# Ranking fourteen experts by load, and giving the six smallest 64-slot steps of plain float32 products

## The chip, the cores and the metric

The kernel runs on one core of one Trainium2 chip. The metric is the device time of one execution in microseconds. The median of three runs of the kernel before is 1223.13 us (1218.1 to 1224.14).

The engines are named as the profile names them: PE multiplies matrices (PEld loads its stationary operands), DVE, ACT and POOL work on elements, SP issues most DMAs. A partition is one of the 128 rows of on-chip memory.

## The reference

A trunk of two layers over 512 tokens of 1024 float32 values. Each layer adds a mixer (layer 0: retention and a state-space model, layer 1: dilated attention; the change touches neither) and then a mixture of 16 experts:

```python
    gval, gsel = lax.top_k(jax.nn.softmax(glog, axis=-1), 1)
...
    elog_sel = jnp.take_along_axis(elog, gsel[:, :, None], axis=1)[:, 0]
    top_v, top_i = lax.top_k(elog_sel, TOP_K)
    top_w = jax.nn.softmax(top_v, axis=-1) * gval
...
    for g in range(N_GROUPS):
        h = jax.nn.silu(jnp.einsum('td,edf->tef', t, w_gate[g])) * jnp.einsum('td,edf->tef', t, w_up[g])
        out = out + jnp.einsum('tef,efd->td', h * combine[:, g, :, None], w_down[g])
```

`glog` and `elog` are the logits of the four groups and of their four experts each. Every token goes to two of the 16 experts, both of one group, so an expert has 64 tokens on average. With the inputs that the reference draws, the 16 experts of layer 0 get 61, 51, 65, 79, 47, 45, 49, 49, 81, 64, 83, 70, 81, 52, 79 and 68 tokens, those of layer 1 get 66, 56, 48, 56, 51, 52, 43, 68, 88, 103, 91, 82, 47, 52, 67 and 54. An expert has three matrices of 1024 x 512 (gate, up) and 512 x 1024 (down), each 2 MB in float32 and read as two loads of 1 MB: 96 loads a layer.

## The kernel before

**Routing.** While the mixer's output projection still runs, the router's logits are worked out chunk by chunk (128 tokens each). `route` then gives each token its place among the rows of its expert (`pos`). `listed(e)` (L966 to L977) turns `pos` into the list of expert e's rows: DVE compares (`oh`, L966), eight short PE products (L972, L973), and a DVE copy to `idx` (L975). A branch (L1270, L1271) sends all work to `moe_any` (every expert over all 512 tokens) if an expert has more than 128 rows.

**Steps.** `moe` (L1086) then runs experts 0 to 15 in the order of their numbers, one step each, always with 128 slots. A step gathers the expert's rows (`fetch`, L1112, an indirect DMA on POOL, issued two steps ahead), turns them with eight transposes into `X` as two tiles (`split_to`, L174), and multiplies in `proj` (L1140 to L1170) by up, then by the next expert's gate, then in `down` by down. Every product is made of three float32r products of 128x512 (`mm3`, L177 to L179): high by high, high by low, low by high. For that every weight block is split: ACT rounds it to the high part, DVE subtracts to get the low part (`wsplit`, with L174). A step so has 24 products, 72 PE instructions of 512 columns, and 12 splits of 128x1024 each on ACT and DVE. `gate` ends in a Silu on ACT (L1174), and L1295 multiplies by up on DVE. The result leaves PSUM on ACT (L1215), and POOL scatters it by an indirect DMA into the rows of `Yd` in HBM (L1216).

**Weights.** SP issues the loads in program order (`load_w`, L235) into a ring of 12 slots of 1 MB, two experts' worth; a load waits until the splits of the slot's last weights are done. The address is constant, the expert's number being known. 14 of a layer's loads are issued before the branch. The second half of up(2) is loaded by POOL (L1154).

**Tail.** Experts 14 and 15 are not scattered: their results stay on chip as high and low parts in `X[0]`, `X[1]`, and `add_rows` (L1237) adds them to `h` by products with one-hot tables, four for each half chunk. The other experts' rows come back from `Yd` by eight loads (L1259) after the last scatter has landed; POOL adds six of them to `h` in layer 0 and four in layer 1 (L1261), DVE and, in layer 1, PE (L1240) the rest.

Of the kernel before, what the change touches and what calls it, by code (L numbers as in the profile page):

```python
# [21 lines left out]
T = 512  # L22
D = 1024
NCH = 4
# [12 lines left out]
C_ID, C_TRI, C_IOTA, C_ZETA, C_TL, C_TIE, C_SEL, C_END = 0, 128, 256, 384, 388, 389, 405, 425  # L37
# [3 lines left out]
def _constants():  # L41
    """Tables that depend on shapes alone."""
# [8 lines left out]
    for i in range(20):  # L51
        cst[i::32, C_SEL + i] = 1.0
    half = 64
# [19 lines left out]
    return {"cst": cst, "tab0": np.ascontiguousarray(tab0), "tab1": np.ascontiguousarray(tab1)}  # L73
# [3 lines left out]
def kernel(ctx: ExitStack, tc: tile.TileContext, I, out, *_):  # L77
# [110 lines left out]
    def sumsq(src, junk, first):  # L188
        """Sums of squares of 512 columns; the first half's is taken with the mean's scale and eps."""
# [12 lines left out]
    scaled, recips = [], []  # L202
# [39 lines left out]
    def wsplit(raw, eng=V):  # L242
        """raw [128, 2, 512]: hi and lo."""
# [43 lines left out]
    def outproj(parts, src, done):  # L287
        """h[t, :] += sum over the two parts (hi, lo, row0) of merged[t, :] src; done(c) after chunk c."""
# [31 lines left out]
    # ---------------------------------------------------------------- layer 0  # L320
# [21 lines left out]
    def s5_tables(st, ld, db, Br, Cn):  # L342
# [36 lines left out]
        M8 = sm.tile([128, 8, 3, 16], F32, bufs=1, name="M8")  # L379
# [92 lines left out]
    def s5_in(hf, W, U, X):  # L472
        """Chunk inputs to states of half hf."""
# [10 lines left out]
    def s5_scan(P, hf, X):  # L484
# [4 lines left out]
        def swap(v):  # L489
            """im before re."""  # L490
# [3 lines left out]
        def step(dst, src, m, n):  # L494
            """dst += lam^(8(m+1)) src; [128, 2, 8, n] views."""
# [243 lines left out]
    # ---------------------------------------------------------------- layer 1  # L739
# [61 lines left out]
    # ---------------------------------------------------------------- mixture of experts  # L801
# [14 lines left out]
    def router_params(l, eng=nc.scalar):  # L816
# [9 lines left out]
        def scaled():  # L826
            """The norm's weights times the router's."""
# [7 lines left out]
    def router(l, wr, br, wrb):  # L835
        grow = rowb(I["ffn_norm"][l])

        def t4(name, *shape, dt=F32):
            return sm.tile([128, NCH] + list(shape), dt, bufs=1, name=name)

        q = SimpleNamespace(r=t4("rank", 5, 4), gs=t4("gs", 4), M=t4("M", NE, dt=BF16), E=[t4(f"E{k}", NE) for k in range(2)],
                            pos=t4("pos", NE), pp=bank(shape=(128, NCH + 1, NE)), oh=t4("oh0", 128, dt=BF16),
                            idx=sm.tile([128, NE, 2], I32, bufs=1, name="idx"), ohf=[], xn=[])
        part = {}

# [6 lines left out]
        def ranks(c):  # L852
            """Rank 3 is the largest of its four, rank 2 the next; the lower index first."""
# [26 lines left out]
        def rows0():  # L880
            """Rows of expert 0 out of the first two chunks; zeros where it has none."""
# [16 lines left out]
        def chunk(c, n):  # L898
            """Half n of chunk c: transposed now, multiplied behind the next half's transposes."""
# [50 lines left out]
    def route(q):  # L950
        M, E, pp, pos, chosen = q.M, q.E, q.pp, q.pos, q.chosen
        for c in range(NCH):
# [8 lines left out]
        def listed(e, part=range(5), oh=None):  # L961
            """Rows of expert e: where they are read from and written to (too large: no row), and their weights."""
            if oh is None:
                oh = ohr[listed.n if listed.n < 2 else 2 * (listed.n % 2)]
                listed.n += 1
                V.tensor_tensor(oh, C[:, C_IOTA:C_IOTA + 128][:, None, :].to_broadcast([128, NCH, 128]),  # L966
                                pos[:, :, e:e + 1].to_broadcast([128, NCH, 128]), op=OP.is_equal)
# [6 lines left out]
            if 0 in part:  # L974
                V.tensor_scalar(idx[:, e, :], pl2[:, 0:2], float(FAR), None, op0=OP.add)  # L975
            if 4 in part:
# [3 lines left out]
        def weights():  # L980
# [28 lines left out]
            V.tensor_tensor(wt, wt, r, op=OP.add)  # L1009
            V.tensor_copy(rc[:, :, :, 2], wt)  # L1010
# [5 lines left out]
        return idx, cmax, M, E, listed, weights, ws  # L1016
# [69 lines left out]
    def moe(l, rt, norm, done):  # L1086
        idx, cmax, M, E, listed, weights, ws = route(rt)
        Yd = Yds[l]
        xg = [F[9][:, 0:1024], F[9][:, 1024:2048]]
# [4 lines left out]
        X, hb = [R[g0]], []  # L1094

        def rest():
            """What the first loads leave: the other expert's rows and the products' operand."""
            X.append(typed(once[0:1], F32R)[0])
# [4 lines left out]
            R[once[0]] = X[1]  # L1103

        def xgb(e):
            return [v3(X[e % 2][:, 1024 * i:1024 * i + 1024], 8) for i in range(2)]
# [3 lines left out]
        def fetch(e):  # L1110
            x_ = xg[e % 2]
            rows[e] = G.indirect_dma_start(out=x_, out_offset=None, in_=xnd[:, :],  # L1112
                                        in_offset=bass.IndirectOffsetOnAxis(ap=idx[:, e, 0:1], axis=0),
                                        bounds_check=T - 1, oob_is_err=False)
# [258 lines left out]
```

## Time and profile before

| | |
|---|---|
| median of three runs | 1223.13 us |
| profiled execution: span | 1223.2 us (no other time of that execution is given) |
| expert steps, layer 0 / layer 1 | 299 to 630 us / 889 us to the end |
| PE, DVE, ACT, POOL busy | 93%, 77%, 60%, 18% of the span |
| DMA, whole span | 284.39 MB, mean 233 GB/s |

The span is the time from the first instruction to the last; it equals the median within 0.1 us. The busy shares are averages over stages with different limits. The two stretches of expert steps are together over half of the span, and the change lies within them, so their rows are read by themselves below.

### The profile page before, as it was taken

What the parts mean: (1) busy time and instruction counts of PE and PEld (TensorE: products, weight loads), DVE (VectorE), ACT (ScalarE), POOL (GpSimd) and SP (SyncE); (2) the same over time, 40 slices, a digit from 0 to 9 for tenths busy, and PEclk for the clock granted to TensorE, in tenths of its full rate; (3) what the DMA queues carried; (4) which work ended last, traced back from release to release, by engine and by line L of the source; (5) the groups of instructions that cost most, each with busy time, mean ns of one, the idle gap of its engine ahead of it and who ended that gap; (6) DMA issues with size and microseconds to landing.
All of it is one profiled execution on the core that took longest, in us unless ns stands there. A gap on an engine that the chain in (4) does not pass through costs nothing. (4 is left out here: it accounts for less than half of the span.)

```text
span 1223.2 us, 16929 instructions
## 1 busy us (share of the span) xinstructions
PE 1135.8 (93%) x6271; PEld 902.6 (74%) x6271; DVE 939.3 (77%) x1497; ACT 729.0 (60%) x1029; POOL 214.4 (18%) x138
## 2 busy tenths in 40 slices
PE   6989797998899999999699999999889999999976
PEld 5767676886678888887468877777667888888754
DVE  5974865766999999988983273275589999999896
ACT  6342144534878888878453353453368888878764
POOL 3553010001211101110620000000032111022041
PEclk9989998998999999999989999999889999999998
DMA  7255532387889999988615314317468999999661
GB/s 240 86 154 203 208 88 94 104 295 232 308 296 342 367 373 351 379 304 278 239 39 173 103 36 172 104 35 258 162 230 307 337 365 371 373 363 382 234 248 69
DMA packets 135745, 284.39 MB, mean 233 GB/s; under 512 B 25067, under 2 KB 25251, under 8 KB 135524
## 3 DMA queue, kind: packets, MB, share of 16 engines
q1 hardware_dynamic: 120564, 248.71, 58.0%
q0 software_dynamic: 9328, 18.63, 4.4%
q10 hardware_dynamic: 5760, 15.86, 3.4%
q8 instruction: 53, 0.87, 0.3%
q14 instruction: 40, 0.33, 0.1%
HBM read 268.74 MB, written 30.41 MB: 245 GB/s over the span
## 5 line engine op out<-in xcount | busy, mean ns | idle before, releaser
L178 PE MATMUL acc<-R,R 128*128 128x512 f32 x1204 | 484.6, 403 | 20.0 <-DVE R L174 19.1
L174 DVE TENSOR_TENSOR R<-F,R 128x1024 fp32r<-128x1024 f32 (+1 forms) x281 | 354.7, 1283 | 127.2 <-ACT R L174 118.0
L177 PE MATMUL acc<-R,R 128*128 128x512 f32 x1084 | 440.7, 408 | 6.7 <-ACT R L174 4.8
L179 PE MATMUL acc<-R,R 128*128 128x512 f32 x1084 | 428.4, 400 | 0.2 <-DVE R L174 0.2
L174 ACT CAST R<-F 128x1024 fp32r<-128x1024 f32 (+1 forms) x284 | 294.6, 1047 | 198.8 <-PE acc L179 102.5
L178 PEld LDWEIGHTS acc<-R,R 128*128 128x128 f32 x1204 | 229.6, 191 | 75.3 <-DVE R L174 26.9
L177 PEld LDWEIGHTS acc<-R,R 128*128 128x128 f32 x1084 | 206.9, 191 | 59.7 <-ACT R L174 15.4
L179 PEld LDWEIGHTS acc<-R,R 128*128 128x128 f32 x1084 | 207.2, 191 | 45.7 <-DVE R L174 1.3
L1112 POOL DMA_INDIRECT F<-xnd,idx x30 | 49.8, 1661 | 346.1 <-DVE idx L975 182.5
L174 DVE TENSOR_TENSOR R<-pb,R 128x512 fp32r<-128x512 f32 x120 | 81.7, 686 | 32.0 <-ACT R L174 31.8
L174 DVE TENSOR_TENSOR R<-R,R 128x1024 fp32r<-128x1024 f32 x70 | 90.2, 1317 | 5.7 <-ACT R L174 5.2
L174 ACT CAST R<-R 128x1024 fp32r<-128x1024 f32 x70 | 72.4, 1053 | 35.9 <-PE acc L179 34.8
L174 ACT CAST R<-pb 128x512 fp32r<-128x512 f32 x120 | 69.8, 589 | 33.9 <-PE pb L170 30.8
L174 DVE TENSOR_TENSOR R<-F,spare 128x1024 fp32r<-128x1024 f32 x58 | 75.1, 1296 | 1.6 <-ACT spare L174 1.5
L174 ACT CAST spare<-F 128x1024 fp32r<-128x1024 f32 x62 | 65.2, 1051 | 9.6 <-PE acc L179 9.2
L179 PE MATMUL acc<-spare,R 128*128 128x512 f32 x180 | 70.9, 394 | 0.0
L177 PE MATMUL acc<-spare,R 128*128 128x512 f32 x180 | 70.5, 392 | 0.0
L1216 POOL DMA_INDIRECT Yd<-m,idx x28 | 35.0, 1252 | 100.8 <-ACT m L1215 94.0
L883 POOL MEMSET R<- 128x1024 f32 x2 | 1.9, 958 | 284.4 <-PE acc L179 284.4
L170 PE MATMUL pb<-C,F 128*128 128x128 f32 x296 | 45.0, 281 | 4.0 <-POOL F L460 3.4
L170 PEld LDWEIGHTS pb<-C,F 128*128 128x128 f32 x296 | 36.2, 145 | 10.7 <-POOL F L460 3.9
L170 PE MATMUL pb<-C,m 128*128 128x128 f32 x164 | 28.4, 295 | 15.3 <-DVE m L207 9.9
(331 smaller groups left out, 1304.7 us busy)
## 6 DMA issues: line engine op xcount, KB each, us to landing
F<-in_moe_w_gate_dram SPq DMA_DIRECT2D x58, 1024.0 KB, 9.1
F<-in_moe_w_down_dram SPq DMA_DIRECT2D x46, 1024.0 KB, 6.8
F<-in_moe_w_up_dram SPq DMA_DIRECT2D x36, 1024.0 KB, 5.0
R<-in_moe_w_up_dram SPq DMA_DIRECT2D x24, 1024.0 KB, 10.2
R<-in_moe_w_down_dram SPq DMA_DIRECT2D x18, 1024.0 KB, 5.7
F<-in_c_w_qkv_dram SPq DMA_DIRECT2D x12, 1024.0 KB, 5.1
F<-in_ab_w_in_dram SPq DMA_DIRECT2D x10, 1024.0 KB, 5.1
Yd<-h ACTq DMA_DIRECT2D x16, 512.0 KB, 4.0
```

What stands on the lines that cost most here:

```text
L170: PE.transpose(dst, src, ident[:n, :n])
L174: return S.copy(hi, src), eng.tensor_tensor(lo, src, hi.bitcast(F32), op=OP.subtract)
L177: PE.matmul(ps, ah, bh, start=first, stop=False)
L178: PE.matmul(ps, ah, bl, start=False, stop=False)
L179: PE.matmul(ps, al, bh, start=False, stop=last)
L883: G.memset(q.x0, 0.0)
L1112: rows[e] = G.indirect_dma_start(out=x_, out_offset=None, in_=xnd[:, :], in_offset=bass.IndirectOffsetOnAxis(ap=idx[:, e, 0:1], axis=0), b ...
L1216: st = G.indirect_dma_start(out=Yd[:, :], out_offset=bass.IndirectOffsetOnAxis(ap=idx[:, e, 1:2], axis=0), in_=y[:, :], in_offset=None, bo ...
```

## The change

`STEPS = "HHHLHHLHLHHLHHLL"` gives each of the 16 steps a kind. Experts 0 and 1 keep the first two steps. The 14 others are ranked on chip by their number of rows: the eight largest go to the heavy steps (H), which are computed as before, the six smallest to the light steps (L: 3, 6, 8, 11, 14, 15), which have 64 slots. The branch to `moe_any` is now also taken if more than eight of the 14 have more than 64 rows.

**Ranking.** `loads` works out the counts and the branch's condition, and PE turns `pos` and `E[1]` together into a transposed tile. After the branch `by_load` ranks the counts on DVE, and two PE products with the resulting permutation give `ids` (the expert's number of each step) and the permuted `pos`. SP reads `ids` into 14 registers; each weight load of a step from 2 on takes its address from one (an ISA instruction ahead of the DMA). The loads of gate(2), issued before the branch so far, now wait for that, and the whole of up(2) is issued by SP.

**Light steps.** Rows are gathered and transposed with 64 partitions. PE's products take float32 operands as they are, with no split of weights or rows. Each is 64 rows by 512 columns, and two at a time are issued to the two column halves of the array: up into PSUM partitions 0 to 63 and gate into 64 to 127 (L1282); the left and the right 512 columns of down (L1302). The scatter writes half rows of 2 KB (L1359).

**Tail.** Steps 14 and 15 are light. Their results stand side by side in one pair of tiles `Z`, 64 slots each, so that `add_rows` has two products where it had four. The four slots that take the rows coming back are now the last four of the ring.

```diff
+STEPS = "HHHLHHLHLHHLHHLL"
...
+            V.tensor_scalar(m14, pp[:, 4, 2:NE], LIGHT + 0.5, CAP / NHEAVY, op0=OP.is_gt, op1=OP.mult)
+            V.tensor_reduce(more, m14, AX.X, OP.add)
+            V.tensor_tensor(cf, cf, more, op=OP.max)
+            V.tensor_copy(cmax, cf)
...
+        def by_load(bT):
+            cnt, rank, own, gt, P = srt[:, 186:187], srt[:, 187:188], srt[:, 142:158], srt[:, 158:172], srt[:, 192:304]
+            V.tensor_tensor(own, srt[:, 112:128], pp[:, 4, :], op=OP.mult)
+            V.tensor_reduce(cnt, own, AX.X, OP.add)
+            V.scalar_tensor_tensor(gt, pp[:, 4, 2:NE], cnt, srt[:, 128:142], op0=OP.subtract, op1=OP.is_gt)
+            V.tensor_reduce(rank, gt, AX.X, OP.add)
+            V.tensor_scalar(P, srt[:, 0:112], rank, None, op0=OP.is_equal)
+            pi = bank(shape=(1, NS))
+            PE.matmul(pi, C[0:64, C_EC:C_EC + 1], P[0:64, 0:NS], start=True, stop=True)
+            ids = srt[0:1, 304:304 + NS].bitcast(I32)
+            V.tensor_copy(ids, pi)
+            pm = bank(shape=(128, 2, NCH, NS))
+            PE.matmul(pm.rearrange("p x c s -> p (x c s)"), bT, P, start=True, stop=True)
+            V.tensor_copy(pos[:, :, 2:NE], pm[:, 0])
...
+            return wv[w][bass.ds(ids[e], 1), r0:r1, :].rearrange("e (k p) n -> p (e k) n", p=128)
...
         def gate(e):
             hs = m2([128, 512], "hs")
-            return hs, S.activation(hs, proj(e, "moe_w_gate"), AF.Silu)
+            if STEPS[e] == "H":
+                return hs, S.activation(hs, proj(e, "w_gate"), AF.Silu)
+            x_, ps = light_x(e), bank(psA, name="acc")
+            for kk in range(2):
+                raw = [load(e, w, kk * 512, kk * 512 + 512) for w in ("w_up", "w_gate")]
+                for k in range(4):
+                    for i in range(2):
+                        PE.matmul(ps[LIGHT * i:LIGHT * i + LIGHT], x_[:, 4 * kk + k, :], raw[i][:, k, :],
+                                  start=kk + k == 0, stop=kk + k == 4, skip_group_check=True)
...
+        def light_down(e, hs):
...
+            for kk in range(2):
+                raw = load(e, "w_down", kk * 256, kk * 256 + 256)
+                for k in range(2):
+                    for i in range(2):
+                        n = 1 - i if flip else i
+                        PE.matmul(ps[LIGHT * i:LIGHT * i + LIGHT], ht[:, 2 * kk + k, :],
+                                  raw[:, k, 512 * n:512 * n + 512], start=kk + k == 0, stop=kk + k == 2,
+                                  skip_group_check=True)
...
+            y = m4([128, 512], "y")
+            S.activation(y, ps, AF.Copy, scale=ws[:, e:e + 1])
+            scattered(G.indirect_dma_start(out=Yh[:, :],
+                                           out_offset=bass.IndirectOffsetOnAxis(ap=idx[:, e, 1:2], axis=0),
+                                           in_=y[:, :], in_offset=None, bounds_check=4 * T - 1, oob_is_err=False))
...
-                    PE.matmul(ps, sel[b][:, c, :], X[b][:, 1024 * i + 512 * n:1024 * i + 512 * n + 512],
-                              start=b == 0 and i == 0, stop=y2 is None and b == 1 and i == 1)
+            for i in range(2):
+                PE.matmul(ps, sel[n][:, c, :], Z(n, i), start=i == 0, stop=y2 is None and i == 1)
...
-                spare.extend(order[5:6] + order[1:4])
-                fr.set(order[0:1] + order[4:5] + order[6:])
+                spare.extend(order[8:12])
+                fr.set(order[0:8])
```

SP's row of instructions before, from the end of the branch in layer 0 (tiles of F and R are slots of the ring, m4, growt and m2w take up(2)):

```order
L1271 UNCONDITIONAL_BRANCH
L1151 DMA m4_0_90<-in_moe_w_up_dram 128x2x512
L1151 DMA growt_107<-in_moe_w_up_dram 128x2x512
L235 DMA F0_70<-in_moe_w_gate_dram 128x4x512
L235 DMA F2_72<-in_moe_w_gate_dram 128x4x512
L235 DMA F3_73<-in_moe_w_down_dram 128x2x1024
```

And SP's row of the changed kernel from the same place:

```order
L1415 UNCONDITIONAL_BRANCH
L1424 TENSOR_LOAD srt_2029
L1177 ISA
L1177 DMA F8_78<-in_moe_w_gate_dram 128x4x512
L1177 ISA
L1177 DMA R3_2494<-in_moe_w_gate_dram 128x4x512
L1253 ISA
L1253 DMA m4_0_90<-in_moe_w_up_dram 128x2x512
L1253 ISA
L1253 DMA growt_107<-in_moe_w_up_dram 128x2x512
L1255 ISA
L1255 DMA m2w_87<-in_moe_w_up_dram 128x4x512
```

The read of `ids` and the two loads of gate(2) now stand ahead of the loads of up(2), and each load has an ISA instruction ahead of it.

PE's row before in layer 0 at the end: the last products of down(15), and the first of `add_rows` (R6, R4, R7 are high and low weights, R2, R0 the results of experts 14 and 15, R1 the operand and the one-hot tables):

```order
L177 MATMUL acc_5275<-R4_2877,R1_2954 128x512
L178 MATMUL acc_5275<-R4_2877,R1_2954 128x512
L179 MATMUL acc_5275<-R4_2877,R1_2954 128x512
L1237 MATMUL acc_5344<-R2_82,R1_2954 128x512 x2
L1237 MATMUL acc_5344<-R0_2953,R1_2954 128x512 x2
L1237 MATMUL acc_5350<-R2_82,R1_2954 128x512 x2
```

And PE's row of the changed kernel at the same place, from the last up and gate products of step 15 on (F are the ring's slots as loaded, R0 the turned rows, m2w the operand of down):

```order
L1282 MATMUL acc_4842<-F3_73,R0_4826 64x512
L1282 MATMUL acc_4842<-F4_74,R0_4826 64x512
L1302 MATMUL acc_4873<-F7_77,m2w_87 64x512 x4
L189 MATMUL pb_4890<-C_92,m2w_87 128x64 x4
L1302 MATMUL acc_4873<-F5_75,m2w_87 64x512 x4
L1302 MATMUL acc_4896<-F6_76,m2w_87 64x512 x4
L1302 MATMUL acc_4896<-F1_71,m2w_87 64x512 x4
L1384 MATMUL acc_4944<-R2_4884,R1_3002 128x512
L1384 MATMUL acc_4948<-R2_4884,R1_3002 128x512 x2
```

PE now reads the weights as they were loaded, with no split between the landing and the products. Behind step 15's up and gate products stand only the sixteen products of down(14) and down(15), then `add_rows`; up(15) and down(15) alone were 48 rows before.

## Rows read from the trace of the kernel before

**Rows 1.** The page: busy time by engine, and GB/s of 40 slices of the span.

```profile
PE 1135.8 (93%) x6271; PEld 902.6 (74%) x6271; DVE 939.3 (77%) x1497; ACT 729.0 (60%) x1029; POOL 214.4 (18%) x138
GB/s 240 86 154 203 208 88 94 104 295 232 308 296 342 367 373 351 379 304 278 239 39 173 103 36 172 104 35 258 162 230 307 337 365 371 373 363 382 234 248 69
```

**Rows 2.** Stretches: us, busy PE, PEld, DVE, ACT, POOL (count), clock, DMA share, GB/s.

```profile
375.00:523.00 148.00, 147.43 (x735) 119.73 (x734) 137.32 (x151) 122.41 (x144) 21.50 (x17) 1.00 1.01 366
523.00:585.20 62.20, 61.98 (x287) 49.14 (x287) 54.46 (x58) 49.87 (x60) 6.11 (x4) 1.00 0.81 283
964.00:1112.00 148.00, 147.42 (x740) 120.62 (x739) 137.93 (x153) 123.10 (x145) 22.66 (x18) 1.00 1.01 369
1112.00:1174.60 62.60, 62.39 (x291) 49.87 (x290) 55.23 (x58) 50.52 (x60) 6.12 (x4) 1.00 0.80 284
493.80:499.00 5.20, 5.20 (x29) 4.20 (x28) 5.05 (x5) 4.95 (x7) 0.00 (x0) 1.00 1.05 399
```

**Rows 3.** POOL's timeline, two scatters of neighbouring steps: start, us, what, idle before.

```profile
427.45 1.01 POOL L1216 DMA_INDIRECT Yd<-m,idx  x1 [0.30 <-issue]
...
446.02 1.00 POOL L1216 DMA_INDIRECT Yd<-m,idx  x1 [0.31 <-issue]
```

**Rows 4.** PE's timeline within a step, three products in a row.

```profile
444.38 0.39 PE L178 MATMUL acc<-R,R 128*128 128x512 f32 x1
444.61 0.39 PE L179 MATMUL acc<-R,R 128*128 128x512 f32 x1
```

**Rows 5.** PE's timeline: float32 products of 512 columns in layer 1's mixer.

```profile
708.03 1.02 PE L759 MATMUL pb<-F,F 128*128 128x512 f32 x2
708.89 0.61 PE L779 MATMUL pb<-m2w,F 128*128 128x128 f32 x4
```

**Rows 6.** PE's timeline: float32 products on column halves (128*64), layer 0's mixer.

```profile
100.60 3.97 PE L479 MATMUL pb<-F,F 128*64 128x64 f32 x128
```

**Rows 7.** PE's timeline: from a full-width product to products on 32 columns.

```profile
281.32 0.39 PE L179 MATMUL acc<-R,R 128*128 128x512 f32 x1
281.64 0.43 PE L917 MATMUL pb<-m,wrb 128*32 128x128 f32 x8
```

**Rows 8.** DMA issues on the page: count, KB each, median us to landing.

```profile
F<-in_moe_w_gate_dram SPq DMA_DIRECT2D x58, 1024.0 KB, 9.1
```

**Rows 9.** DVE's timeline behind layer 0's branch.

```profile
299.05 0.69 DVE L966 TENSOR_TENSOR m2w<-C,pos 128x512 bf16<-128x512 f32 x1 [2.84 <-PEq L1271]
299.66 0.15 DVE L975 TENSOR_SCALAR idx<-pb 128x2 int32<-128x2 f32 x1
```

**Rows 10.** PE's timeline, end of layer 0's steps, with waits.

```profile
599.54 0.50 PE L178 MATMUL acc<-R,R 128*128 128x512 f32 x1 [1.67 <-DVE R L174]
...
611.24 1.11 PE L170 MATMUL pb<-C,m 128*128 128x128 f32 x4 [3.62 <-DVE m L1295]
...
613.62 0.63 PE L178 MATMUL acc<-R,R 128*128 128x512 f32 x1
614.05 0.63 PE L177 MATMUL acc<-R,R 128*128 128x512 f32 x1
...
621.07 6.13 PE L1237 MATMUL acc<-R,R 128*128 128x512 f32 x26
...
629.31 0.40 PE L177 MATMUL acc<-R,R 128*128 128x512 f32 x1
```

**Rows 11.** POOL's timeline, end of layer 0's steps.

```profile
577.46 1.83 POOL L1216 DMA_INDIRECT Yd<-m,idx  x1 [19.36 <-ACT m L1215]
588.98 6.11 POOL L1261 TENSOR_TENSOR h<-h,F 128x1024 f32<-128x1024 f32 x2 [9.69 <-DMA F<-Yd]
...
601.69 6.68 POOL L1261 TENSOR_TENSOR h<-h,F 128x1024 f32<-128x1024 f32 x2
```

**Rows 12.** SP's timeline: the first loads of the rows coming back, layer 0.

```profile
585.22 0.82 SPq L1259 DMA_DIRECT2D F<-Yd  x2
```

**Rows 13.** PE's timeline, end of layer 1's steps.

```profile
1205.26 6.62 PE L1237 MATMUL acc<-R,R 128*128 128x512 f32 x28
```

More of the change, by code (lines that the diff above doesn't have):

```diff
@@ L52, in _constants @@
         cst[i::32, C_SEL + i] = 1.0
+    e_ = p % 16
+    e2 = np.arange(2, 16)
+    th = np.where(e2[None, :] < e_[:, None], -0.5, 0.5)
+    heavy, light = iter(range(NHEAVY)), iter(range(NHEAVY, NS))
+    rank = [next(heavy) if k == "H" else next(light) for k in STEPS[2:]]
+    blk = np.full((128, 8, NS), -1.0)
+    for i in range(128):
+        if i % 16 >= 2:
+            blk[i, i // 16] = rank
+    own = (np.arange(16)[None, :] == e_[:, None]).astype(np.float32)
+    srt = np.concatenate([blk.reshape(128, 112), own, th], 1).astype(np.float32)
+    cst[:, C_EC] = e_
+    cst[:, C_HF] = FAR + 0.5 * (p >= 64)
     half = 64
@@ L1014, in weights @@
             return wt
-        return idx, cmax, M, E, listed, weights, ws
+        return idx, cmax, M, E, listed, weights, ws, loads, by_load
     def moe_any(l, M, E, wt, buf):
@@ L1086, in moe, with rows_of, load @@
     def moe(l, rt, norm, done):
-        idx, cmax, M, E, listed, weights, ws = route(rt)
+        idx, cmax, M, E, listed, weights, ws, loads, by_load = route(rt)
         Yd = Yds[l]
+        Yh = Yd.rearrange("r (h d) -> (r h) d", h=2)
+        wv = {w: I["moe_" + w][l].rearrange("g e d f -> (g e) d f") for w in ("w_gate", "w_up", "w_down")}
+        ids = {}
+        def rows_of(e, w, r0, r1):
+            if e < 2:
+                return wv[w][e, r0:r1, :].rearrange("(k p) n -> p k n", p=128)
+            return wv[w][bass.ds(ids[e], 1), r0:r1, :].rearrange("e (k p) n -> p (e k) n", p=128)
+        def load(e, w, r0, r1):
+            t = v3(F[fr.next()], (r1 - r0) // 128)
+            fr.load = nc.sync.dma_start(t, rows_of(e, w, r0, r1))
+            return t
         xg = [F[9][:, 0:1024], F[9][:, 1024:2048]]
@@ L1181, in down @@
             evac = split_to(hh, hl, pt)
-            src = I["moe_w_down"][l, e // 4, e % 4]
-            raw = [load_w(src[kk * 256:(kk + 1) * 256, :], 2) for kk in range(2)]
+            raw = [load(e, "w_down", kk * 256, kk * 256 + 256) for kk in range(2)]
             ps = [bank(psA, name="acc") for _ in range(2)]
@@ L1193, in down @@
                         mm3(ps[n], hh[:, k, :], hl[:, k, :], wh[:, i, :], wl[:, i, :], k == 0, k == 3)
-            if e == NE - 1:
-                with after(wsplit.hi.ins):
-                    table(AF.Sqrt)
-            if e >= NE - 2:
-                b = e % 2
-                V.tensor_tensor(wl2[:, b:b + 1], ws[:, e:e + 1], cf, op=OP.mult)
-                for n in range(2):
-                    hi, lo = (X[b][:, 1024 * i + 512 * n:1024 * i + 512 * n + 512] for i in range(2))
-                    last = [S.activation(hi, ps[n], AF.Copy, scale=wl2[:, b:b + 1]),
-                            V.scalar_tensor_tensor(lo, ps[n], wl2[:, b:b + 1], hi.bitcast(F32), op0=OP.mult, op1=OP.subtract)]
-                nxt.append(last)
-                return
             if e == 0:
@@ L1220, in scatter, with tokens @@
             scat.append(st)
[L1222 removed]
+        def tokens(n):
             idf = sm.tile([128, 1], F32, name="idf")
[L1225 to L1226 removed]
+            for i in range(2):
+                sl = slice(LIGHT * i, LIGHT * i + LIGHT)
+                V.tensor_copy(idf[sl], idx[sl, NE - 2 + (i != n), 0:1])
+            p = v3(R[9][1][:, 512 * n:512 * n + 512], 4)
             for c in range(NCH):
@@ L1275, in moe @@
         R[wrs[2]] = typed(wrs[2:], F32R)[0]
-        for e in (1, 2):
-            listed(e, range(2))
-            fetch(e)
+        perm, row = by_load(bT)
+        listed(1, range(2))
+        fetch(1)
         listed(0, range(2), rt.oh)
+        _, vals = nc.values_load_multi_w_load_instructions(
+            row[0:1, :], engines=(mybir.EngineType.SP,), min_val=0, max_val=NE - 1,
+            skip_runtime_bounds_check_because="sums of one-hot rows: each is one of 2 to 15, or 0")
+        ids.update(zip(range(2, NE), vals))
+        listed(2, range(2))
+        fetch(2)
         m2r.set([4, 5])
@@ L1285, in moe @@
         rest()
-        weights()
+        weights(perm)
         m2r.set([5, 4])
@@ L1298, in moe @@
                 hs, silu = gate(e + 1)
+            if e == NE - 2:
+                with after(silu.ins):
+                    table(AF.Sqrt)
             late = down(e, cur)
@@ L1305, in moe @@
                 spread()
-            if e == NE - 2:
-                wr_.set([i for i in (wr_.next() for _ in range(4)) if i != 9])
             if e == NE - 3:
                 order = [fr.next() for _ in range(12)]
-                spare.extend(order[5:6] + order[1:4])
-                fr.set(order[0:1] + order[4:5] + order[6:])
+                spare.extend(order[8:12])
+                fr.set(order[0:8])
             if e == NE - 1:
-                for i, t in zip(raws, typed(raws, F32R)):
+                for i, t in zip(raws + once[0:1], typed(raws + once[0:1], F32R)):
                     R[i] = t
-                with after(wsplit.lo.ins):
-                    sel = [tokens(i) for i in (e - 1, e)]
+                sel = [tokens(n) for n in range(2)]
                 y2 = combine_rest()
```

148 lines of the change are left out of this document (110 added, 38 removed).

## The prediction

> **What bounds the kernel now.** I read the page's busy shares first [rows 1]: PE is busy for 93% of the span, so the question is what sets PE's pace in the expert steps. The table of stretches [rows 2] answers for the middle of both layers: in 375 to 523 us PE is busy for 147.4 of 148 us at clock 1.00, DVE for 137.3. But the same row shows the DMA share at 1.01 and 366 GB/s, the like stretch of layer 1 has 369. So two resources are full at once. From one scatter to the next a step takes 446.02 - 427.45 = 18.57 us [rows 3]. PE's 512-column products start 0.23 us apart [rows 4]; 72 of them are 16.7 us, and the 1.87 us left are transposes and the lists' short products. In these 18.57 us the DMAs bring 6 loads of 1.049 MB, 6.3 MB, and at 369 GB/s move 6.85 MB in all: the rest, 0.55 MB, is gather and scatter. A load takes 9.1 us to land [rows 8], so more than two are always under way.
>
> Whether the DMAs have room beyond that, the rows don't say at once, since PE asks for no more than it gets. In 5 us without a gather they moved 399 GB/s at share 1.05 [rows 2]. With share 1.01 and gathers and scatters within, I take **369 GB/s as what they can do in steady state**, and 399 as the upper bound.
>
> The ends of the steps are another stage. There the DMAs have run at 283 GB/s (share 0.81) for 62 us before the last expert [rows 2], and PE then waits for splits: 1.67 us at a time for DVE, 3.62 once, with the clock going down behind it (products 0.43 us apart at 613.62) [rows 10], while POOL adds the rows that came back [rows 11].
>
> **The change part by part.**
>
> *Light step on PE.* Out go 72 products of 0.23 us. In come 24 products of 64x512 in float32, in 12 pairs. A float32 product of 512 columns is two instructions, and the next work starts 0.86 us after it (708.03 to 708.89) [rows 5]. Do the two halves of a pair run beside each other? The nearest row has 128 instructions of 64 columns on column halves in 3.97 us, 0.031 us each [rows 6]. Alone, one of 512 columns took 0.43 us, so one of 64 would take 0.43 x 64/512 = 0.054. In pairs they so go at 1.7 times the pace of single ones, the last one's end included, and I take a pair for 0.86 us; without overlap it is 1.72. Twelve pairs are 10.3 us. Of the 1.87 us of transposes and lists I keep 1.2, as transposes now have 64 columns. A light step is **11.5 us on PE in place of 18.6**, 7 us less, and six of them 42 us less per layer (bound: 21.9 us without overlap).
>
> The float32 products want no splits, so 12 of DVE's and of ACT's per light step go. DVE was busy for 93% of the steady stretch [rows 2]; where a light step stands between heavy ones it has room now.
>
> Going into the half-width products may cost something. The rows have one such change: 0.32 us from a full-width start to the 32-column products, against 0.23 to the next full-width one [rows 7, 4], so 0.09 us at most. Some six changes in a light step are 0.5 us, 3 us a layer, and only where PE binds.
>
> *DMA.* The light steps read the same 6 MB. So their 18.6 us of transfers stay when PE's part falls to 11.5: the DMAs become the bound, and PE will wait for weights. The gain is what the DMAs left unused. In layer 0 they moved 148 x 366 = 54.2 MB from 375 to 523 us and 62.2 x 283 = 17.6 MB on to 585.2, the end of the weights' stretch [rows 2]. These 71.8 MB take 194.6 us at a steady 369 GB/s: from 375 the last weight lands at about 570, plus 3 us for the later start (below), **573** (at 399 GB/s 558). PE's products of down(15) ended at 621.07 before [rows 10]; now only the last half of down(15) stands behind the landing, two pairs or 1.7 us, and PE is done at about 576. The waits may bring the lower clock, as behind 611.24 [rows 10]; with one light step among three PE has 7 us to spare (18.6 + 18.6 + 11.5 against three times 18.6), so within the steps I count none of it.
>
> Here a figure of the Trainium skill speaks against the change. Its page DMA: Bandwidth & Descriptors, section Specifications, puts the HBM limit of a core at about 358 GB/s. By that the 71.8 MB would take 200.6 us, 6 us more, as would those of layer 1, and the sum would be 1182. The rows have 366 and 369 GB/s over 148 us, so the measurement stands above that figure and decides; the time by the figure is an estimate that lies within the bounds of the forecast below.
>
> *Start.* Ranking adds some eight small DVE operations, nearest row 0.15 us [rows 9], two PE products, and a read of the registers by SP. I take 3 us in series after the branch (between 1 and 5). Behind SP's read of the registers stand all loads from gate(2) on, and behind the new list of step 2 its gather on POOL. gate(2) is multiplied behind five sets of 8 products (gate 0, up 0, gate 1, down 0, up 1), 5 x 24 x 0.23 = 28 us at least, so PE doesn't wait; the DMAs start the rest 3 us later. SP issues a load in 0.41 us [rows 12], six in a step of 18.6, so the ISA instruction ahead of each is hidden by SP's idle time; should SP fall behind, it costs that instruction once per load. POOL loses a load that it issued, at 18% busy [rows 1] nothing.
>
> *Scatter and gather.* A light gather has 64 indices in place of 128, a scatter 128 half rows. The rows that exist are the same number, so the bytes stay; nearest row for the issue is 1.0 us on POOL [rows 3], hidden. Six loads at 399 GB/s are 15.8 us of the 18.6, so gather and scatter take some 2.8 us of the DMAs; I take that to stay, and as the bound half as much again, 1.4 us a step.
>
> *Tail, layer 0.* What is late next is the rows coming back. Their loads were issued at 585.22, 7.8 us after the last scatter at 577.46, and POOL's six adds of 3.1 to 3.3 us went from 588.98 to 608.4 [rows 12, 11], hidden by PE until 621. Now step 13 ends some 20 us ahead of the last landing, so the loads are queued behind the last weights; they are 8 of 0.5 MB, 11 us at 369 GB/s. The first lands at about 576, and POOL ends 6 x 3.2 = 19 us later, 596. Then come the additions of the last two chunks and the norm: I take 6 us (`add_rows` took 8.2 us before, 621.07 to 629.31, with twice the products) [rows 10]. Layer 0 ends at about **602 in place of 629.3: 27 us**.
>
> *Tail, layer 1.* 62.6 x 284 = 17.8 MB in 1112 to 1174.6 take 48.2 us at 369: 14.4 us earlier, less 3 for the start: the last weight at about 1163, PE done at 1166. POOL has four adds, to about 1180. Before, the end came 1223.2 - 1205.26 = 18 us after the products of the last expert [rows 13]; now these 18 us start at 1166 but wait until about 1180 for the rows of the middle chunks, which I take to leave 17 us: **1197, 26 us**.
>
> **Sum:** 1223 - 27 - 26 = **1170 us**, against a span that equals the median.
>
> **Rivals.**
>
> *A, the forecast: DMA becomes the bound,* 1160 to 1185 by 380 to 355 GB/s.
>
> *B: the DMAs keep up.* For it speaks the 399 GB/s of rows 2; against it share 1.01 at 366 in the long stretches. Then PE's 7 us times five steps and a gate come off before 585, and the end of down(15) is near 562; POOL's adds end near 584, the layer at 589: 40 us per layer, **1140**. The Trainium skill, page DMA: Bandwidth & Descriptors, section Bandwidth, gives 425 GB/s for a core alone in transfers of 16 MB; by that it would be this rival, but the rows above show no more than 399.
>
> *C: the DMAs get worse,* by the gathers and scatters of other shapes or by loads that SP issues later. With 1.4 us more in each of the eleven steps after 375, 15 us per layer, **1200**.
>
> *D: the halves don't overlap.* A light step is 21.9 us on PE, 3.3 more than now. Six are 20 us per layer, while the tail's waits for splits (some 21 us between 587 and 621) go: about **1220**. Rows 6 speak against it.
>
> *E, slower: the branch goes the other way.* If more than eight of 14 experts have over 64 rows, a layer runs `moe_any`. Layer 0 has just eight, with one expert at 64 sharp. At least 64 x 24 products at 0.86 us are 1,320 us for that layer: **over 2,400**. It decides at one token more; against it speaks that the counts of the drawn inputs stay within.
>
> **How the numbers follow.** A 0.72 (1170), B 0.10 (1140), C 0.10 (1200), D 0.05 (1220), E 0.03. The range takes in A, most of B and C: 1136 to 1206. A measurement of this kernel can tell about 0.5%, 6 us. Faster by more than that: A, B, C, nearly all, and part of D: 0.92; within 0.5%: most of D, 0.05; slower: E, 0.03.
>
> **What would show it.** Light products (L1282, L1302) should start 0.43 us apart in pairs; twice that is D. From 380 to 573 us the DMA share should stay at 1.0 and GB/s near 369, also where it was 283; if it falls below 0.95 there, B. PE's waits in steps 6, 8, 11 should be for loads of F, not for DVE. DVE's share should fall from 93% to near 65%. The waits for splits behind 587 should be gone, and POOL's adds be the last thing before `add_rows` ends. I am wrong in kind if PE waits early, before 375, for registers or gate(2), or if the steady rate lies under 355 GB/s.

## The result, and the profile after

The changed kernel took 1166.67 us (median of four, 1165.98 to 1167.94) against 1223.64 for the kernel before in the same measurement: 0.9539 of it, 95% interval 0.9517 to 0.9561. The forecast was 1170. The profiled execution has a span of 1164.8 us, 58.4 less than before; layer 1 begins at 601.07 in place of 629.31 [rows 10], 28.2 us earlier, and the other 30.2 us come in layer 1.

The page after, the line that answers to the first of [rows 1], and a line on weight loads that answers to [rows 8]:

```profile
PE 1067.4 (92%) x5967; PEld 769.2 (66%) x5967; DVE 747.7 (64%) x1369; ACT 571.4 (49%) x857; POOL 201.7 (17%) x136
...
F<-in_moe_w_gate_dram SPq DMA_DIRECT2D x52, 1024.0 KB, 15.4
```

DVE went from 77% to 64%, ACT from 60% to 49%, PE only from 93% to 92%: the span fell along with PE's work. A weight load now lands 15.4 us after its issue, not 9.1: more of them are under way at a time. The stretches show where that begins. Columns as in [rows 2] (us, busy PE, PEld, DVE, ACT, POOL with counts, clock, DMA share, GB/s):

```profile
336.00:375.00 39.00, 38.30 (x206) 26.68 (x205) 31.05 (x40) 25.43 (x31) 6.75 (x4) 1.00 0.80 292
375.00:490.00 115.00, 114.61 (x589) 79.21 (x588) 82.67 (x103) 72.54 (x88) 23.28 (x17) 1.00 1.03 385
490.00:575.00 85.00, 79.39 (x342) 46.30 (x343) 44.24 (x62) 40.42 (x50) 6.93 (x6) 0.96 0.94 347
```

From 375 us on the DMAs move 385 GB/s where they moved 366, at share 1.03. But PE has no gap in these 115 us: 114.61 busy. PE's pauses come only behind 490: 79.39 of 85 busy there. A light step on PE's timeline (start, us, line, operation), gate and up first, then the rows' transposes; and its two halves of down:

```profile
360.10 7.09 PE L1282 MATMUL acc<-F,R 128*64 128x512 f32 x32
367.11 0.66 PE L189 MATMUL pb<-C,m 128*128 128x128 f32 x4
...
381.88 1.94 PE L1302 MATMUL acc<-F,m 128*64 128x512 f32 x8
383.65 1.89 PE L1302 MATMUL acc<-R,m 128*64 128x512 f32 x8
385.47 0.50 PE L196 MATMUL acc<-R,R 128*128 128x512 f32 x1
```

Sixteen products (32 instructions) take 7.01 us from their start to the next group's, 0.44 us for two that run beside each other, and down 385.47 - 381.88 = 3.59 us. The 12 pairs are 10.6 us, the forecast had 10.3.

PE's timeline again, where it first has to wait (numbers in brackets are idle time and what ended it):

```profile
489.85 1.07 PE L1282 MATMUL acc<-F,R 128*64 128x512 f32 x2
490.86 0.66 PE L189 MATMUL pb<-C,m2w 128*128 128x128 f32 x4
491.35 0.38 PE L189 MATMUL pb<-C,F 128*128 128x128 f32 x2
491.66 3.65 PE L1282 MATMUL acc<-F,R 128*64 128x512 f32 x14
...
497.38 3.65 PE L1282 MATMUL acc<-F,R 128*64 128x512 f32 x14
502.42 0.40 PE L189 MATMUL pb<-C,m2w 64*128 64x64 f32 x3 [1.40 <-DVE m2w L1285]
...
521.66 0.49 PE L196 MATMUL acc<-R,R 128*128 128x512 f32 x1 [1.72 <-ACT R L193]
522.91 0.80 PE L197 MATMUL acc<-R,R 128*128 128x512 f32 x1 [0.76 <-DVE R L193]
523.51 0.63 PE L198 MATMUL acc<-R,R 128*128 128x512 f32 x1
523.93 0.63 PE L196 MATMUL acc<-R,R 128*128 128x512 f32 x1
```

This light step's up and gate do not stand in one row as those at 360.10 did. They are split into 2, 14, 2 and 14 instructions, with the transposes and lists of other steps between them, and the two at 489.85 take 1.01 us until the next group starts, where two in a row took 0.44. The first wait is for the light step's own Silu and multiplication, which end behind its last product. The second is for a split on ACT. What ACT did before that split (its timeline):

```profile
519.98 0.69 ACT L1358 ACTIVATE m<-acc,ws 128x512 f32<-128x512 f32 x1 [3.00 <-PE acc L1302]
520.57 1.98 ACT L193 CAST R<-R 128x1024 fp32r<-128x1024 f32 x2
```

ACT was held by the step before: it waited 3.00 us for PE's own down products (L1302) and took them out of PSUM. It was not waiting for a landing. All waits of PE from 375 to 600 us, in its list of waits (engine, line, what for, us, times, longest):

```profile
PE pb L189 <- DVE m L226: 3.1, 2, 2.0
PE pb L189 <- DVE m2w L1285: 2.8, 2, 1.4
PE acc L1384 <- ACT R L1314: 2.3, 1, 2.3
PE acc L196 <- ACT R L193: 1.7, 1, 1.7
PE acc L197 <- DVE R L193: 1.0, 2, 0.8
PE acc L1384 <- DVE h L1388: 0.9, 1, 0.9
PE acc L1302 <- DVE m2w L1295: 0.2, 1, 0.2
```

None of them was ended by a landing, and the like list of layer 1 has none either. The list of all engines from 375 to 575 us has one wait of a split for a landing:

```profile
ACT R L193 <- DMA R<-in_moe_w_down_dram: 3.3, 1, 3.3
```

It ended at 438.68, where PE had no gap.

Behind 522.91 the products run 0.42 us apart for a while, the granted clock having fallen to its lower level (0.50 in 523 to 526 us). And the end of the layer's steps, PE's timeline and then POOL's:

```profile
571.07 6.65 PE L1282 MATMUL acc<-F,R 128*64 128x512 f32 x29
...
580.18 5.37 PE L1302 MATMUL acc<-F,m2w 128*64 128x512 f32 x24
587.83 3.14 PE L1384 MATMUL acc<-R,R 128*128 128x512 f32 x12 [2.27 <-ACT R L1314]
...
601.07 1.22 PE L196 MATMUL acc<-R,R 128*128 128x512 f32 x2 [0.95 <-ACT R L193]
```

```profile
572.14 0.97 POOL L1352 DMA_INDIRECT Yd<-m,idx  x1 [26.81 <-ACT m L1351]
579.24 4.79 POOL L1407 TENSOR_TENSOR h<-h,F 128x1024 f32<-128x1024 f32 x2 [6.14 <-DMA F<-Yd]
583.99 9.62 POOL L1407 TENSOR_TENSOR h<-h,R 128x1024 f32<-128x1024 f32 x4
```

SP's timeline has the last four loads, of down:

```profile
548.88 7.40 SPq L1177 DMA_DIRECT2D F<-in_moe_w_down_dram  x4
```

The last of them is issued at 555.3 and, with the 14.5 us that its like took, lands at about 570. The last half of up and gate of step 15 was issued by 545.35 and with a median of 15.4 us lands at about 561, 10 us before PE comes to step 15. From 571 to 585.6 PE works off what has landed, with hardly a wait. So the weights lay there before PE wanted them: by this trace PE's own row of work sets the end, not the landings. The waits for splits of [rows 10] are gone.

### The profile page after: what moved, and what is told of

Same layout as the page of the kernel before. It is cut to its first block, busy times and chain, and to the rows that moved or that the text cites. A ratio compares the mean times of both kernels' runs of the same rounds, so it can differ in the third digit from the quotient of the medians.

```text
span 1164.8 us, 16185 instructions
## 1 busy us (share of the span) xinstructions
PE 1067.4 (92%) x5967; PEld 769.2 (66%) x5967; DVE 747.7 (64%) x1369; ACT 571.4 (49%) x857; POOL 201.7 (17%) x136
## 5 line engine op out<-in xcount | busy, mean ns | idle before, releaser
L197 PE MATMUL acc<-R,R 128*128 128x512 f32 x936 | 379.9, 406 | 12.1 <-DVE R L193 12.1
L196 PE MATMUL acc<-R,R 128*128 128x512 f32 x860 | 350.9, 410 | 18.1 <-ACT R L193 7.0
L198 PE MATMUL acc<-R,R 128*128 128x512 f32 x860 | 344.2, 403 | 3.0 <-DVE R L193 3.0
L193 DVE TENSOR_TENSOR R<-F,R 128x1024 fp32r<-128x1024 f32 (+1 forms) x185 | 223.9, 1229 | 143.2 <-ACT R L193 135.1
L193 ACT CAST R<-F 128x1024 fp32r<-128x1024 f32 (+1 forms) x188 | 193.0, 1040 | 187.7 <-PE acc L198 95.0
L197 PEld LDWEIGHTS acc<-R,R 128*128 128x128 f32 x936 | 179.2, 191 | 57.5 <-DVE R L193 19.5
L196 PEld LDWEIGHTS acc<-R,R 128*128 128x128 f32 x860 | 164.8, 192 | 62.6 <-ACT R L193 13.0
L198 PEld LDWEIGHTS acc<-R,R 128*128 128x128 f32 x860 | 165.1, 192 | 39.2 <-DVE R L193 4.8
L1282 PE MATMUL acc<-F,R 128*64 128x512 f32 x336 | 92.7, 598 | 0.0
L1282 PEld LDWEIGHTS acc<-F,R 128*64 128x64 f32 x336 | 26.7, 136 | 48.4 <-issue 47.3
L189 PE MATMUL pb<-C,F 128*128 128x128 f32 (+1 forms) x296 | 41.6, 274 | 7.1 <-DVE F L226 3.7
L196 PE MATMUL acc<-spare,R 128*128 128x512 f32 x116 | 45.8, 395 | 0.0
L198 PE MATMUL acc<-spare,R 128*128 128x512 f32 x116 | 45.6, 393 | 0.0
L189 PEld LDWEIGHTS pb<-C,F 128*128 128x128 f32 (+1 forms) x296 | 31.7, 147 | 19.4 <-issue 12.1
L193 DVE TENSOR_TENSOR R<-F,spare 128x1024 fp32r<-128x1024 f32 x34 | 41.5, 1220 | 2.3 <-ACT spare L193 2.1
## 6 DMA issues: line engine op xcount, KB each, us to landing
F<-in_moe_w_gate_dram SPq DMA_DIRECT2D x52, 1024.0 KB, 15.4
F<-in_moe_w_down_dram SPq DMA_DIRECT2D x42, 1024.0 KB, 14.5
```

The lines of the kernel that those rows point to most:

```text
L189: PE.transpose(dst, src, ident[:n, :n])
L196: PE.matmul(ps, ah, bh, start=first, stop=False)
L197: PE.matmul(ps, ah, bl, start=False, stop=False)
L198: PE.matmul(ps, al, bh, start=False, stop=last)
L1282: PE.matmul(ps[LIGHT * i:LIGHT * i + LIGHT], x_[:, 4 * kk + k, :], raw[i][:, k, :], start=kk + k == 0, stop=kk + k == 4, skip_group_check= ...
```

## The experiments

Theory 1 was that of the forecast: behind the first steps the landing of weights sets the end. Its rival, theory 2: PE's own work sets it all along. A third reading was not among the expectations: PE's work and its waits depend on the order in which its instructions stand, and most of the edits below change that order as well. Each run is the changed kernel with the edit shown; ratios are to the kernel before in the same measurement.

**Half the loads of light steps.** Down likewise.

```diff
-                raw = [load(e, w, kk * 512, kk * 512 + 512) for w in ("w_up", "w_gate")]
+                raw = [load(e, w, 0, 512) for w in ("w_up", "w_gate")] if kk == 0 else raw
```

> The changed kernel, but a light step loads only the first half of its three matrices (3 MB in place of 6) and multiplies by that half twice: PE's work is as before, and part of the result is wrong by intention. Theory 1 (from about 375 us on the DMAs set the pace, PE waits for weights behind about 490 us): 18 MB less per layer, 47 us at 381 GB/s; PE's pauses and the low clock behind them go, some 13 to 17 us per layer, and the time falls to 1133 to 1143. Theory 2 (PE sets the pace all along, the pauses are chance): 1160 to 1167.

1138.52 us (0.930, 0.9281 to 0.9319), 28 us less than the changed kernel, 14 per layer. PE had the same products to do. The same two stretches as above:

```profile
375.00:490.00 115.00, 114.61 (x591) 79.05 (x591) 84.92 (x103) 73.89 (x89) 24.29 (x17) 1.00 0.97 358
490.00:575.00 85.00, 81.40 (x385) 48.23 (x382) 44.91 (x65) 42.98 (x55) 16.78 (x11) 0.98 0.71 258
```

Until 490 nothing changed for PE, though the DMAs brought less: there PE was its own bound. Behind 490 PE executes 385 instructions in place of 342 and gains 12 us on the changed kernel (down(15) ends at 572.5 in layer 0, not at 585.6). But the run differs in two things: the bytes, and the order on PE. The light step that the changed kernel has split from 489.85 on stands in one row here:

```profile
488.87 7.09 PE L1282 MATMUL acc<-F,R 128*64 128x512 f32 x32
```

The changed kernel's waits for Silu and for the split, 5.3 us of idle time, are gone. Since the changed kernel had no wait for a landing, this number fits theory 1 but does not show it; a run with all loads and this order on PE is missing.

**Half the products of light steps.** All loads stay.

```diff
-                for k in range(4):
+                for k in range(2):
```

> The changed kernel with all its loads, but a light step leaves out every second of its products (12 of 24), so PE has 5.3 us less to do in each, 32 us less per layer; the result is wrong by intention. Theory 1 (the DMAs set the pace): the last weight of layer 0 lands at about 569 us as before, only the products behind it get shorter, 15 us of PE to 8: 1150 to 1156. Theory 2 (PE sets the pace): the landings come earlier with the slots, and most of 32 us per layer is gained: 1105 to 1130.

1152.66 us (0.9412, 0.9385 to 0.9439): 14 us less, 7 per layer, where PE lost 32 us of work per layer. The DMAs go on at 371 to 382 GB/s and share 1.0 or more in both stretches, PE idles instead, and now it does wait for landings (the two stretches, and PE's timeline at the end of layer 0's steps):

```profile
375.00:490.00 115.00, 107.05 (x531) 75.17 (x531) 81.08 (x99) 69.99 (x86) 21.63 (x16) 0.99 1.03 382
490.00:575.00 85.00, 70.72 (x308) 41.75 (x306) 46.33 (x66) 44.25 (x56) 7.62 (x7) 0.96 1.00 371
...
566.33 1.08 PE L1302 MATMUL acc<-F,m2w 128*64 128x512 f32 x4 [0.23 <-DMA F<-in_moe_w_down_dram]
572.13 1.97 PE L1302 MATMUL acc<-F,m2w 128*64 128x512 f32 x4 [1.36 <-DMA F<-in_moe_w_down_dram]
```

PE is done at 574.1, 2 us behind the last wait for a landing and 11 us sooner than in the changed kernel. So the end that the DMAs set lies, by this estimate, some 11 us ahead of PE's end in the changed kernel, and most of the 32 us could not be gained. This is theory 1's number, for a kernel with less work on PE.

**Only the last two steps light.**

```diff
-STEPS = "HHHLHHLHLHHLHHLL"
+STEPS = "HHHHHHHHHHHHHHLL"
```

> Only the last two steps (14, 15) are light, the twelve others heavy: the tail, the ranking and the register addresses without the four light steps in the middle. Theory 1: between 375 and 540 us the DMAs had no room before either, so the four inner light steps are worth little (5 to 10 us per layer): 1177 to 1190. Theory 2: an inner light step is worth its 6 us of PE, 24 us per layer: 1210 to 1220.

1187.16 us (0.9695, 0.9673 to 0.9718). The two light steps at the end are worth about 37 us of the 57, and the four inner ones, with 26 to 28 us of PE work saved per layer, bring 20.5 together, 10 per layer. In the middle of that kernel PE has no gap either, with the DMAs at 370 GB/s:

```profile
375.00:490.00 115.00, 114.58 (x569) 93.05 (x568) 106.88 (x120) 95.39 (x112) 18.35 (x15) 1.00 1.01 370
```

The number is theory 1's, but the full DMAs are not shown to be the reason. Against the run with half the loads, whose light steps stand in one row, the four inner ones are worth 48.6 us, 24 per layer, nearly all that they save PE; but that run differs in its bytes too.

**Light steps last.**

```diff
+STEPS = "HHHHHHHHHHLLLLLL"
```

> The same number of heavy and light steps, but the six light ones are the last (10 to 15). PE's work and the bytes are the same. Theory 1: the DMAs are full either way, so the last weight lands at about 569 us again; but light products can follow a landing at once where heavy ones wait for a split, so PE ends 3 to 5 us behind it in place of 17: 1140 to 1155. Theory 2 (PE's work sets the end): 1162 to 1170.

1162.64 us (0.9491, 0.9472 to 0.951): by its number theory 2, by its trace theory 1. In this run PE waits for landings, 11.5 us in the two layers together. PE does follow the last landing closely, as expected, and ends at 578.3 (PE's timeline, last products of down):

```profile
576.39 1.94 PE L1302 MATMUL acc<-F,m 128*64 128x512 f32 x8 [0.53 <-DMA F<-in_moe_w_down_dram]
```

But the weights land some 5 us later, since heavy steps at the start take only 364 GB/s. And the returning rows come behind them: POOL's adds (its timeline) begin at 577.77, 1.5 us sooner than in the changed kernel, and so the layer ends at 598.5, only 2.6 us sooner, though PE was done 7 us sooner.

```profile
375.00:490.00 115.00, 114.64 (x572) 93.10 (x571) 107.21 (x122) 94.75 (x111) 19.26 (x14) 1.00 1.02 364
...
577.77 4.80 POOL L1407 TENSOR_TENSOR h<-h,F 128x1024 f32<-128x1024 f32 x2 [18.38 <-DMA R<-Yd]
```

My expectation had missed both. By the ratios this order is some 0.5% faster than the changed kernel (0.9491 to 0.9539); the two were not timed side by side.

**Light steps early.** STEPS = "HHHLLLHHLHHHHHLL".

> The same number of heavy and light steps, but light ones at 3, 4, 5, 8, 14, 15. Theory 1: three light steps in a row empty the ring of 12 slots, PE waits for landings there already; the last weight lands at 565 to 570 us in layer 0 since the DMAs are full from 370 us on either way; five heavy steps in a row at 18.6 us then make PE late: 1165 to 1178. Theory 2 (PE's work alone sets the time): 1165 to 1168 with no waits in the light steps.

1162.46 us (0.9522, 0.9505 to 0.9538), the time of the changed kernel within the intervals, and below the span that I expected. PE waits earlier (110.30 of 115 us busy from 375 to 490) and less later (82.76 of 85), at 391 and 351 GB/s. None of its waits was ended by a landing. Where the light steps stand moves the waits more than the time.

**Up and gate one after the other.**

```diff
-                        PE.matmul(ps[LIGHT * i:LIGHT * i + LIGHT], x_[:, 4 * kk + k, :], raw[i][:, k, :],
+                        PE.matmul((ps, pg)[i][0:LIGHT], x_[:, 4 * kk + k, :], raw[i][:, k, :],
```

> The changed kernel with up and gate of a light step written to the same 64 PSUM partitions of two banks, so that no two of its products use different column halves; down stays in halves. If the halves run beside each other in the changed kernel, gate and up of a light step take 13.8 us in place of 7.0 on PE, a light step some 19 in place of 12 to 13, and PE sets the pace again: of 41 us per layer more on PE some 15 take the place of waits, 1210 to 1225. If the halves never ran beside each other: 1165 to 1170.

1214.97 us (0.9951, 0.9934 to 0.9969): the gain is nearly gone. PE's timeline shows 13 instructions in 5.67 us up to the next group, 0.44 each where two took that long:

```profile
369.63 5.74 PE L1282 MATMUL acc<-F,R 128*64 128x512 f32 x13
375.30 0.66 PE L189 MATMUL pb<-C,m 128*128 128x128 f32 x4
```

So the halves do run beside each other in the changed kernel, and without that the plain float32 step is hardly worth anything.

**Constant addresses.** The numbers of the experts for these inputs written into the addresses, no registers.

```diff
-            return wv[w][bass.ds(ids[e], 1), r0:r1, :].rearrange("e (k p) n -> p (e k) n", p=128)
+            return wv[w][ids[e], r0:r1, :].rearrange("(k p) n -> p k n", p=128)
```

> The changed kernel with the experts' numbers of these inputs written in as constants for the load addresses; the ranking itself stays. No register read on SP, no ISA instruction ahead of a load, and the loads need not wait for the ranking. Theory 1 (the DMAs set the end, so 3 to 4 us later at the start are 3 to 4 us at the end; the addressing itself is free): 1158 to 1164. Rival (registers make each load's issue slower and cost more than the start): under 1155. Rival (the start is hidden by the loads in flight): 1165 to 1168.

1155.08 us (0.9464, 0.9444 to 0.9483), 11.6 us less than the changed kernel by the medians, 9 by the ratios. It lies between theory 1's range and that of the first rival, and is more than I had counted, 3 us a layer. But four things differ. The two loads of gate(2) are issued ahead of the branch again: in 275 to 305 us the DMAs move 233 GB/s in place of 176, 1.7 MB more. The next norm's weights and up(5) have other places on SP's queue. No instruction stands ahead of a load. And PE has another order, with the light step at 490 in one row:

```profile
488.79 7.09 PE L1282 MATMUL acc<-F,R 128*64 128x512 f32 x32
...
581.16 2.12 PE L1384 MATMUL acc<-R,R 128*128 128x512 f32 x8 [2.28 <-ACT R L1314]
```

Up to there PE is only 1.1 us ahead of the changed kernel (488.79 to 489.85), at the end of down(15) 6.7 us (578.9 to 585.6). So most of the gain arises where PE's order differs, and what the register addresses cost by themselves is not shown. The next two runs try the places on the queue.

**The norm's load later.** Behind down(5) in place of down(3).

> The changed kernel with one load moved on SP's queue: that of the next norm's weights into growt, issued behind down(5) in place of down(3). In the changed kernel it stands ahead of up(4) (in the kernel before and in the run with constant addresses behind it), waits until up(2) has left growt, and up(4) is issued at 354.64 us in place of 346.92. Theory: that place on the queue is what the run with constant addresses gained, the register addresses cost nothing: 1154 to 1159. Rival: the ISA instructions and the later start are what it gained: 1164 to 1168.

1166.64 us (0.9547, 0.9521 to 0.9573): no change at all. up(4) was issued at 347.54 as expected, and the next loads, which wait for their slots, at 363.61 as before. PE's order is that of the changed kernel.

**up(5) first.** As the run before, and up(5) ahead of gate(5) and down(4) on SP's queue.

> The changed kernel with register addresses, the norm's load behind down(5), and SP's queue as it stood in the run with constant addresses: up(5) is issued ahead of gate(5) and down(4), into the slots it has anyway, which come free at 359 us where gate(5)'s come free at 363. Theory (order on SP's queue is what the run with constant addresses gained, a load that waits for its slot holds up others whose slots are free): the second place was this one, 1155 to 1160. Rival (that run gained by the two loads of gate(2) that it issued ahead of the branch, or by the missing ISA instructions): 1164 to 1168.

1170.69 us (0.9559, 0.9535 to 0.9583). The DMAs moved more from 336 to 375, 325 GB/s in place of 292 (321 with constant addresses), but the time did not fall. Both theories of the queue's order fell with that. PE's order is that of the changed kernel here too. What is left are the loads ahead of the branch, the instructions ahead of the loads, and PE's order; no run separates them.

**Light steps from step 2 on.** STEPS = "HHLHHLHLHHLHHHLL".

> The same number of heavy and light steps, light ones at 2, 5, 7, 10, 14, 15 in place of 3, 6, 8, 11, 14, 15 (up(2) then goes through the ring, with no extra buffers). In the changed kernel the DMAs run at only 292 GB/s from 336 to 375 us, because heavy steps hold the slots. Theory 1 (the DMAs set the end): the slots come free earlier, the last weights land 6 to 10 us earlier per layer: 1148 to 1158. Theory 2 (PE's work sets the end): only the DVE-bound start of step 2 gets shorter: 1160 to 1165.

1183.56 us (0.9695, 0.9675 to 0.9716), slower than the changed kernel. In this layout three operand tiles share two buffers, so part of its output is another, and I blamed the buffers for the time; the next run has six.

> Light steps at 2, 5, 8, 11, 14, 15, the norm's load behind down(5), and six buffers for the products' operands from step 2 on, since the run with a light step at 2 had two and its products waited for them. Theory 1 (the DMAs set the end): they are full from about 340 us on in place of 370 and the weights land up to 10 us earlier per layer: 1140 to 1152. Rival (PE's work sets the end once the queue no longer blocks): 1153 to 1160.

1187.54 us (0.9702, 0.9674 to 0.9731): it was not the buffers. The DMAs did start as expected, 364 GB/s from 336 to 375 us in place of 292. Behind 375 the gain was lost: PE waits there already (110.83 of 115 us busy from 375 to 490), and none of its waits was ended by a landing. Its light steps at 8 and 11 both stand split on PE.

> As the run before, with light steps at 2, 5, 8, 13, 14, 15: three light ones at the end. Theory 1: the last weights land as in the run before, and PE ends closer behind them, but the rows of the scattered experts then come back last, as in the run with six light steps at the end: 1140 to 1155, within 5 us of the run before. Rival (PE's work sets the end): the same time as the run before within 2 us.

1169.7 us (0.9568, 0.9544 to 0.9592), 18 us faster than the run before with one light step at 13 in place of 11. That contradicts my expectation that the two would lie within 5 us. In these layouts up(2) goes through the ring and no longer has buffers of its own, 2 MB less that can be loaded ahead; whether that or PE's order is what they lose by is only argued, and remains open.

## Why the prediction was right, step by step

The time was right, the cause that it named was not: PE did not wait for weights. That 1170 came out is luck.

- **Light step on PE:** right. The pair takes 0.44 x 2 = 0.88 us with its two passes (forecast 0.86), a light step's products 10.6 (10.3). DVE's share fell to 72% in 375 to 490 us, not to the 65% that followed from longer steps. That rested on [rows 5, 6]; the run with up and gate in turn shows the other end.
- **The DMAs become the bound, and PE will wait for weights:** wrong. The rate was 385 GB/s over 115 us, not the 369 that I had read from [rows 2] as a limit; that was what the steps then asked for. Up to 490 us PE had no wait, and behind it none of its waits was ended by a landing. They were for the light step's own Silu (1.40 us twice) and for a split that ACT came to late (1.72 and 0.76), as PE's instructions stand there. The sum for the DMAs was good in itself: with half the products PE waited for its last landing until 572.1, where the forecast had 573.
- **The Trainium skill's figure:** the page DMA: Bandwidth & Descriptors, section Specifications, has 358 GB/s from HBM for a core, a stack's rate halved between two cores. This trace moved 385 over 115 us with one core at work, so the figure is no limit here; the 425 of its section Bandwidth was not reached either.
- **The last landing:** forecast 573, measured about 570. The higher rate brought less than it might, since from 560 to 570 us the DMAs moved 281 GB/s only.
- **PE 1.7 us of work behind the last landing:** wrong, and it follows from the step above. PE ended at 585.6, not 576. It was still at step 15's up and gate and both downs (571.07 to 585.6) when everything had landed. The forecast took it for granted that PE keeps up, since a light step leaves it 7 us to spare, and counted neither the waits within a light step nor the lower clock behind them.
- **Tail, layer 0:** the end came at 601.07, forecast 602, by two errors against each other: PE 9.6 us later, and a shorter tail. POOL's adds took 2.4 us each and not 3.2 [rows 11], and ended at 593.6. Between PE's end and the layer's end lay 15.5 us in place of the 26 I had counted.
- **Tail, layer 1:** 30.2 us gained, forecast 26. PE was done 21.7 us before the end, where the forecast had 31.
- **Start:** 3 us forecast. The scatter of step 0 came at 336.04 where the like one before was at 332.25, 3.8 us later. With constant addresses it came at 335.30, so 0.7 us of that went with the registers and the loads that came later. Whether they cost more at the end is open.
- **Rivals:** B had the mechanism, PE's pace, and by the prediction's own sign (a share below 0.95) the 0.94 behind 490 speaks for it. Its 1140 is the time of the run with half the loads (1138.5), but the changed kernel took 27 us more. C is refuted: the DMAs moved more per us, not less. D is refuted by the run with up and gate in turn. E did not occur, since the branch was not taken.

In the changed kernel PE is thus slower than B assumed, by its waits, the low clock and its split light steps, and that made up for a bound that PE did not reach. How much of it the order alone costs, and why the order differs between the runs, stays open.

## What to carry to other kernels

A transfer rate at full share is no proof of a limit while the consumer sets its pace: the share was 1.01 at 366 GB/s and 1.03 at 385. To find who sets the pace, look at what ended the consumer's waits, and at when the last bytes landed and when they were used: here they lay there for some 10 us. Taking away half of the bytes in one run and half of the work in another helps, but compare the order of instructions before you read such a run; if that changed too, the run tests two things at once.

## What the runs showed of the hardware that I had not expected

POOL's addition of 128x1024 float32 takes 2.40 us (4.79 for two) when DVE is not splitting, and 3.06 to 3.34 us when it is [rows 11]. The Trainium skill, page GPSIMD Engine Reference, section Specifications, states that GpSimd's interfaces to on-chip memory are shared with VectorE and contend with its instructions that read two such inputs, as the splits do; the rows agree. And while the DMAs run at full share (1.03 in 375 to 490 us) the issue itself takes long: two loads on SP's timeline took 7.29 us to issue, where two took 0.82 in [rows 12].

```profile
444.18 7.29 SPq L1177 DMA_DIRECT2D F<-in_moe_w_gate_dram  x2
```
